# Both projections of a hybrid decoder layer as seven block products for eight, with heads one by one

## The chip, the cores and the metric

The kernel runs on one core of one Trainium2 chip. The metric is device time in microseconds (us) of one execution. Five engines work in parallel, each on its own queue of instructions: TensorE (PE, matrix products; its weight loads are shown as PEld), VectorE (DVE), ScalarE (ACT), GpSimd (POOL) and SyncE (SP, which here only issues DMAs). Sixteen DMA engines move the data that these queues ask for.

## The reference

One layer for 512 tokens and a model width of 2048, all in float32:

```python
h = rms_norm(x, norm_gain)
z = h @ w_in                        # 2048 -> 8192 columns, eight groups of 1024
q_h, f_h, i_h, g_h, q_a, k_a, v_a, g_a = split(z)
y_h = hgrn2_mixer(q_h, f_h, i_h) * silu(g_h)               # 8 heads of 128, chunks of 64 tokens
y_a = dilated_attention_mixer(q_a, k_a, v_a) * silu(g_a)   # 16 heads of 64
x = x + concat(y_h, y_a) @ w_out    # 2048 -> 2048
out = rms_norm(x, final_gain)
```

The HGRN2 mixer is a gated linear recurrence: a running product of the gates within a chunk, masked scores of 64 by 64, a state of 128 by 128 carried from chunk to chunk, and a norm per head. The attention is causal with a bias per head, and its three dilation patterns are merged into one count of how often a key is seen.

## The kernel before, in words

Each float32 operand of the two projections is cut in two float32r pieces: `hi` is a rounded copy (ScalarE) and `lo` the rest, source minus `hi` (VectorE, in places GpSimd). A product of two tiles is then three matmuls, hi by hi, hi by lo and lo by hi (`bank_step`, L134), each of a 128 x 128 stationary tile by 512 moving columns.

The 512 tokens' normed input stays in SBUF as 16 tiles `hh`, `hl` of 128 x 512, transposed (`split_h`, L174); the row norm is applied later, when a result leaves PSUM, so the products can start before it is known. It comes from squares that ScalarE makes and GpSimd adds up (`square_h`, `row_stats`, `row_stats_along`), while products run.

The columns of `w_in` are taken in chunks (L29): for each half of the HGRN heads the chunks `hq`, `hf`, `hg`, `hv` of 512 columns, that is four heads at a time, then for each half of the attention heads `av` with 512 columns and four chunks `ap` of 3 x 128 columns, one pair of heads each. A chunk is four (or three) PSUM banks filled over 8 weight tiles of 512 (384) KB, which are loaded on SP's queue five ahead (`load_w`) and cut three ahead (`split_w`). Values and gates of HGRN come out with tokens in the partitions, the rest with features there.

The mixers' work is strewn among the products: a `tick` stands ahead of each bank's share of a weight tile, and `at_slot(n, ...)` hangs a piece of a mixer on the n-th tick from there (`work_hf` and `work_hv` for HGRN, `work_ap` for a pair of attention heads). That is the order in the text; the framework's planner may still let a later instruction whose operands it expects to be ready go ahead of an earlier one on the same engine.

The mixers' outputs `yT` stay in SBUF, are cut (`split_y`) and go through `w_out` in two halves: first the eight HGRN tiles for all four column groups, then the eight attention tiles, each time four banks by 512 columns, with the residual `x` added when a bank is emptied. Squares for the last norm are taken group by group (`residual`), and the last 128 tokens are done in two halves of 256 columns so that the end is short (L657 to L663).

Of the kernel before, what the change touches and what calls it, by code (L numbers as in the profile page):

```python
# [8 lines left out]
F32 = mybir.dt.float32  # L9
# [4 lines left out]
PSUM = bass.MemoryType.PSUM  # L14

P = 128
S = 512
D = 2048
KT = D // P
NSB = S // P  # L20
HEADS_H = 8
HEADS_A = 16
CH = 64
# [5 lines left out]
def _chunks():  # L29
    out = []  # L30
    for g in range(2):
        for kind, base in (("hq", 0), ("hf", 1024), ("hg", 3072), ("hv", 2048)):
            out.append((kind, g, [(base + 512 * g, 512)]))
    for g in range(2):
        out.append(("av", g, [(4096 + 2048 + 512 * g, 512)]))
        for j in range(4 * g, 4 * g + 4):
            out.append(("ap", j, [(4096 + 128 * j, 128), (4096 + 1024 + 128 * j, 128),
                                  (4096 + 3072 + 128 * j, 128)]))
    return out


CHUNKS = _chunks()
# [3 lines left out]
def tile_kernel(ctx: ExitStack, tc: tile.TileContext, x, xT, w_in, w_out, gain, lbl, gnorm, fgain,  # L46
# [5 lines left out]
    wp = ctx.enter_context(tc.tile_pool(name="wp", bufs=2))  # L52
    pp = ctx.enter_context(tc.tile_pool(name="pp", bufs=4, space=PSUM))
    mx = ctx.enter_context(tc.tile_pool(name="mx", bufs=4, space=PSUM))
    yp = ctx.enter_context(tc.tile_pool(name="yp", bufs=1))

    def open_pool(name, side="left"):
        cm = tc.tile_pool(name=name, bufs=1, side=side)
        return cm, cm.__enter__()
# [4 lines left out]
    def mixer_bank(name):  # L64
        return mx.tile([P, 512], F32, tag="mx", name=name)

# [12 lines left out]


    offs = []
    o = 0
    for _, _, cols in CHUNKS:
        offs.append(o)
        o += 16 * P * sum(c for _, c in cols)

    stream = []
    for ci, (_, _, cols) in enumerate(CHUNKS):
        width = sum(c for _, c in cols)
        stream += [(w_in, offs[ci] + j * P * 2 * width, width) for j in range(8)]  # L90
    out_at = len(stream)
    out_order = [(n, j) for n in range(4) for j in range(4)] + [(n, j) for n in range(4) for j in range(4, 8)]
    stream += [(w_out, (n * 8 + j) * P * 2 * 512, 512) for n, j in out_order]
    raws, splits = [], []
    last_at = len(stream) - 4
    wl = {}

    def load_w(upto):
        while len(raws) < min(upto, len(stream)):
            i = len(raws)  # L100
            src, s0, width = stream[i]
            src = src[s0:s0 + P * 2 * width].rearrange("(p t c) -> p t c", p=P, t=2)
            raw = wp.tile([P, 2, width], F32, tag="raw", name=f"raw_{i}", bufs=5)
            if i == 0:
                nc.scalar.dma_start(raw[:, 0], src[:, 0])
                nc.sync.dma_start(raw[:, 1], src[:, 1])
            else:
                nc.sync.dma_start(raw, src)
            raws.append(raw)

    def split_w(upto):
        while len(splits) < min(upto, len(stream)):
            i = len(splits)
            width = stream[i][2]
            his, los = [], []
            for t in range(2):
                if i >= last_at:
                    hi = wl["pool"].tile([P, width], F32R, name=f"hi_{i}_{t}")
                    lo = wl["pool"].tile([P, width], F32R, name=f"lo_{i}_{t}")
                else:  # L120
                    hi = wp.tile([P, width], F32R, tag="hi", name=f"hi_{i}_{t}", bufs=6)
                    lo = wp.tile([P, width], F32R, tag="lo", name=f"lo_{i}_{t}", bufs=6)
                if i == 0:
                    V.tensor_copy(hi, raws[i][:, t])
                else:
                    A.copy(hi, raws[i][:, t])  # L126
                on_pool = i == 0 or (t == 1 and i < out_at and CHUNKS[i // 8][0] in ("hg", "hv"))
                (G if on_pool else V).tensor_sub(lo, raws[i][:, t], hi.bitcast(F32))  # L128
                his.append(hi)
                los.append(lo)  # L130
            splits.append((his, los))


    def bank_step(tokens_out, ps, b, k0, w, first, last, sh, sl, cols=slice(None)):  # L134
        c = slice(b * P, (b + 1) * P)
        for t in range(2):
            k, hi, lo = k0 + t, w[0][t][:, cols], w[1][t][:, cols]
            st_, en = first and t == 0, last and t == 1
            if tokens_out:
                T.matmul(ps, sh[k][:, c], hi, start=st_, stop=False)  # L140
                T.matmul(ps, sh[k][:, c], lo, start=False, stop=False)  # L141
                T.matmul(ps, sl[k][:, c], hi, start=False, stop=en)  # L142
            else:
                T.matmul(ps, hi[:, c], sh[k], start=st_, stop=False)  # L144
                T.matmul(ps, hi[:, c], sl[k], start=False, stop=False)  # L145
                T.matmul(ps, lo[:, c], sh[k], start=False, stop=en)  # L146
# [7 lines left out]

    yT = [yp.tile([P, S], F32, tag=f"y{k}", name=f"yT{k}") for k in range(8)]
    atv = ctx.enter_context(tc.tile_pool(name="atv", bufs=1))
    hp_cm, hp = open_pool("hp")
    hh, hl = [None] * KT, [None] * KT
    for k in reversed(range(KT)):
        hh[k] = hp.tile([P, S], F32R, tag=f"hh{k}", name=f"hh{k}")  # L160
        hl[k] = hp.tile([P, S], F32R, tag=f"hl{k}", name=f"hl{k}")
    st_cm, st = open_pool("st", "right")
    acc = st.tile([P, S], F32, name="acc")

    xts = []

    def load_x(upto):
        while len(xts) < min(upto, KT):
            k = len(xts)
            xt = st.tile([P, S], F32, tag="xt", name=f"xt_{k}", bufs=8)  # L170
            nc.sync.dma_start(xt, xT[k * P:(k + 1) * P, :])
            xts.append(xt)

    def split_h(k):  # L174
        xt = xts[k]
        A.activation(hh[k], xt, AF.Copy, scale=gain_sb[:, k:k + 1])  # L176
        V.scalar_tensor_tensor(hl[k], xt, gain_sb[:, k:k + 1], hh[k].bitcast(F32), op0=ALU.mult, op1=ALU.subtract)

    def square_h(k):
        if k == 0:  # L180
            A.activation(acc, xts[k], AF.Square)
        else:
            sq = st.tile([P, S], F32, tag="sq", name=f"xsq_{k}", bufs=3)
            A.activation(sq, xts[k], AF.Square)
            G.tensor_add(acc, acc, sq)

    cs = {}

# [12 lines left out]
    def small_consts():  # L201
        cc = cst.tile([P, 256], F32, name="cc")
        nc.sync.dma_start(cc, consts[:, :256])
# [6 lines left out]
        cs["gnorm"] = cst.tile([P, P], F32, name="gnorm_sb")  # L210
        nc.sync.dma_start(cs["gnorm"], gnorm[0:1, :].to_broadcast([P, P]))
        lt = cst.tile([P, 2, HEADS_H], F32, name="lt")
        nc.sync.dma_start(lt, lbl)
# [10 lines left out]
        cs["omlb"] = cst.tile([P, HEADS_H], F32, name="omlb")  # L224
        V.tensor_scalar(cs["omlb"], cs["lb"], -1.0, 1.0, op0=ALU.mult, op1=ALU.add)
        for name, half in (("hlb", 0.5), ("nhlb", -0.5)):
            cs[name] = cst.tile([P, HEADS_H], F32, name=name)
            V.tensor_scalar(cs[name], cs["omlb"], half, None, op0=ALU.mult)

    def row_stats():  # L230
# [9 lines left out]
        cs["hrstd"] = cst.tile([P, NSB], F32, name="hrstd")  # L240
        V.tensor_scalar(cs["hrstd"], rstd, 0.5, None, op0=ALU.mult)

    def row_stats_along():

        rstd = cs["rstd"]
        bank = mixer_bank("rrow_ps")
        for sb in range(NSB):
            dg = st.tile([P, P], F32, tag="dg", name=f"dg_{sb}", bufs=2)
            V.tensor_scalar(dg, cs["ident"], rstd[:, sb:sb + 1], None, op0=ALU.mult)
            T.matmul(bank[:, sb * P:(sb + 1) * P], cs["ones"], dg, start=True, stop=True)  # L250
        cs["rrow"] = cst.tile([P, S], F32, name="rrow")
        A.copy(cs["rrow"], bank)


    H = {}

    def open_hg():
        H["cm"], H["hg"] = open_pool("hg", "right")
# [6 lines left out]
    def evac_hq(g, banks):  # L265
        H["q"] = []
        for b, ps in enumerate(banks):
            q = H["hg"].tile([P, S], F32, tag="q", name=f"q_{g}_{b}", bufs=4)
            V.scalar_tensor_tensor(q, ps, 0.5, cs["rrow"], op0=ALU.mult, op1=ALU.mult)
            H["q"].append(q)  # L270
            at_slot(b + 1, silu, q, H["hg"], f"q_{g}_{b}")

    def silu(s, pool, name):

        t = pool.tile([P, S], F32, tag="t", name=f"t_{name}", bufs=2)
        A.activation(t, s, AF.Tanh)
        V.scalar_tensor_tensor(s, t, 1.0, s, op0=ALU.add, op1=ALU.mult)

    def evac_hf(g, banks):
        fs = []  # L280
        for b, ps in enumerate(banks):
            f = H["hg"].tile([P, S], F32, tag="f", name=f"f_{g}_{b}", bufs=4)
            V.tensor_mul(f, ps, cs["rrow"])
            fs.append(f)
        H["f"] = fs
        H["aux"] = [None] * 4
        for b in range(4):
            work_hf(g, b, H["q"][b], fs[b], H["aux"])

    def work_hf(g, b, q, f, aux):  # L290
# [444 lines left out]
```

## Time and profile before

| | us |
|---|---|
| median of 3 runs | 999.63 (999.51 to 1000.3) |
| the profiled execution | 999.73 |
| its span, first to last instruction | 998.0 |
| PE busy | 978.2 (98%) |
| DVE busy | 541.7 (54%) |
| ACT busy | 397.2 (40%) |
| POOL busy | 167.0 (17%) |

The page's first part gives busy time by engine. A busy PE is not PE at its peak: matmuls overlap, so the time that one costs is the distance from its start to the next start in the timeline, not its own duration. The chain of waits is followed back from the last instruction and says which engine's work set the end. The windows view gives busy time of each engine in a stretch, and the DMA part what the queues moved.

### The profile page before, as it was taken

The numbers are of one execution on the slowest core, as the hardware profiler recorded it, in microseconds if no ns is written. First come the engines' busy times: TensorE is split into PE (matmuls) and PEld (weight loads), VectorE is DVE, ScalarE is ACT, GpSimd is POOL, SyncE is SP. The second block draws the span as 40 slices with busy tenths as digits, with TensorE's granted clock in tenths as the row PEclk, the third lists the DMA queues.
The fourth block names the chain that finished last, engine by engine and source line by source line (L and its number), as shares of the span: only waits on it lengthen the run. The fifth ranks groups of instructions, "written<-read, shape, count | busy, mean of one in ns | idle before, by whom it ended". The sixth has DMA issues, their size and how long they took to land.

```text
span 998.0 us, 12703 instructions
## 1 busy us (share of the span) xinstructions
PE 978.2 (98%) x4704; PEld 799.6 (80%) x4704; DVE 541.7 (54%) x1107; ACT 397.2 (40%) x764; POOL 167.0 (17%) x150
## 2 busy tenths in 40 slices
PE   5999999999999999999999999999999999999996
PEld 4888888888888888888878778788787877888885
DVE  7752883245439813543765666326666686443533
ACT  5531543323334423242554454334444464213413
POOL 6500354011013620111000010000100100001220
PEclk8999999999999999999999999999999999999998
DMA  8422223311222332123222232133222362332304
GB/s 293 147 96 97 77 101 107 106 64 64 96 95 72 110 114 79 49 69 104 87 79 80 90 106 68 51 92 96 79 80 85 106 254 100 112 103 88 106 1 169
DMA packets 31486, 99.08 MB, mean 99 GB/s; under 512 B 3632, under 2 KB 3904, under 8 KB 30784
## 3 DMA queue, kind: packets, MB, share of 16 engines
q1 hardware_dynamic: 30528, 92.76, 28.2%
q0 software_dynamic: 752, 5.25, 1.3%
q8 instruction: 37, 0.61, 0.3%
q10 hardware_dynamic: 144, 0.26, 0.1%
q14 instruction: 25, 0.20, 0.1%
HBM read 94.06 MB, written 4.19 MB: 98 GB/s over the span
## 4 chain that ended last, share of the span: by engine, by line
PE 97%; ACT 1%; DVE 0%; DMA 0%; issue 0%; ACTq 0%; POOLq 0%; DVEq 0%
PE pp L144 15%; PE pp L146 15%; PE pp L145 14%; PE pp L140 9%; PE pp L142 9%; PE pp L141 9%; PE pq L140 3%; PE pq L142 3%; PE pq L141 3%; PE po L140 3%; PE po L141 3%; PE po L142 3%; PE ao L507 2%; PE p L498 2%; PE s L484 1%; PE s L483 1%
## 5 line engine op out<-in xcount | busy, mean ns | idle before, releaser
L128 DVE TENSOR_TENSOR lo<-raw,hi 128x512 fp32r<-128x512 f32 (+1 forms) x318 | 217.9, 695 | 266.9 <-ACT hi L126 215.8
L126 ACT CAST hi<-raw 128x512 fp32r<-128x512 f32 (+1 forms) x350 | 201.2, 581 | 377.2 <-PE pp L145 143.4
L144 PE MATMUL pp<-hh,hi 128*128 128x512 f32 x640 | 258.9, 406 | 6.3 <-ACT hh L176 6.1
L146 PE MATMUL pp<-hh,lo 128*128 128x512 f32 x640 | 251.7, 394 | 4.8 <-DVE lo L128 4.8
L145 PE MATMUL pp<-hl,hi 128*128 128x512 f32 x640 | 251.2, 393 | 0.0
L140 PE MATMUL pp<-hi,hh 128*128 128x512 f32 x384 | 152.2, 396 | 0.0
L142 PE MATMUL pp<-hi,hl 128*128 128x512 f32 x384 | 149.7, 390 | 0.0
L141 PE MATMUL pp<-lo,hh 128*128 128x512 f32 x384 | 149.6, 390 | 0.0
L146 PEld LDWEIGHTS pp<-hh,lo 128*128 128x128 f32 x640 | 121.2, 189 | 32.4 <-DVE lo L128 6.0
L144 PEld LDWEIGHTS pp<-hh,hi 128*128 128x128 f32 x640 | 121.6, 190 | 30.4 <-ACT hh L176 6.1
L145 PEld LDWEIGHTS pp<-hl,hi 128*128 128x128 f32 x640 | 121.9, 191 | 22.0
L142 PEld LDWEIGHTS pp<-hi,hl 128*128 128x128 f32 x384 | 72.1, 188 | 15.4
L140 PEld LDWEIGHTS pp<-hi,hh 128*128 128x128 f32 x384 | 72.1, 188 | 14.6 <-issue 0.3
L141 PEld LDWEIGHTS pp<-lo,hh 128*128 128x128 f32 x384 | 72.2, 188 | 13.8
L128 POOL TENSOR_TENSOR lo<-raw,hi 128x512 fp32r<-128x512 f32 x34 | 47.9, 1412 | 139.7 <-ACT hi L126 127.3
L489 ACT ACTIVATE pr<-pr,sm 128x128 f32<-128x128 f32 (+1 forms) x64 | 36.0, 563 | 72.2 <-DVE sm L487 72.2
L475 POOL TENSOR_SCALAR nb<-dist 128x512 f32<-128x512 f32 x16 | 9.9, 620 | 324.8 <-DVE sm L487 316.1
L140 PE MATMUL pq<-hi,yh 128*128 128x512 f32 (+1 forms) x136 | 52.0, 382 | 0.0
L141 PE MATMUL pq<-lo,yh 128*128 128x512 f32 (+1 forms) x136 | 52.0, 382 | 0.0
L142 PE MATMUL pq<-hi,yl 128*128 128x512 f32 (+1 forms) x136 | 52.0, 382 | 0.0
L140 PE MATMUL po<-hi,yh 128*128 128x512 f32 x128 | 51.0, 398 | 0.0
L142 PE MATMUL po<-hi,yl 128*128 128x512 f32 x128 | 49.9, 390 | 0.0
(153 smaller groups left out, 1098.8 us busy)
## 6 DMA issues: line engine op xcount, KB each, us to landing
raw<-w_in_dram SPq DMA_DIRECT2D x79, 512.0 KB, 3.3
raw<-w_in_dram SPq DMA_DIRECT2D x64, 384.0 KB, 3.0
raw<-w_out_dram SPq DMA_DIRECT2D x32, 512.0 KB, 3.3
xt<-xT_dram SPq DMA_DIRECT2D x16, 256.0 KB, 5.7
r<-x_dram POOLq DMA_DIRECT2D x4, 1024.0 KB, 8.9
out_dram<-r SPq DMA_DIRECT2D x16, 256.0 KB, 2.7
fg<-fgain_dram POOLq DMA_DIRECT2D x1, 1024.0 KB, 5.2
dist<-consts_dram SPq DMA_DIRECT2D x1, 512.0 KB, 4.5
```

The lines of the kernel that those rows point to most:

```text
L126: A.copy(hi, raws[i][:, t])
L128: (G if on_pool else V).tensor_sub(lo, raws[i][:, t], hi.bitcast(F32))
L140: T.matmul(ps, sh[k][:, c], hi, start=st_, stop=False)
L141: T.matmul(ps, sh[k][:, c], lo, start=False, stop=False)
L142: T.matmul(ps, sl[k][:, c], hi, start=False, stop=en)
L144: T.matmul(ps, hi[:, c], sh[k], start=st_, stop=False)
L145: T.matmul(ps, hi[:, c], sl[k], start=False, stop=False)
L146: T.matmul(ps, lo[:, c], sh[k], start=False, stop=en)
L483: T.matmul(s_ps[:, :L], Q[i][:, qc], KH[i][:, :L], start=True, stop=False)
L489: A.activation(p[:, :L], p[:, :L], AF.Exp, bias=sm[:, 0:1], scale=-1.0, accum_out=sm[:, 1:2])
L498: T.transpose(p_ps[:, c], pr[i, qb][:, c], cs["ident"])
L507: T.matmul(o_ps[64 * i:64 * i + 64, kb * P:], vs[kb][:, hc], PT[i][:, kb, kb * P:], start=kb == 0, stop=kb == 3)
```

## The change

The two projections are done by a scheme of Strassen's kind. Tokens are halved (2 x 256), the 2048 inner rows are halved, and the output columns are taken in pairs of blocks. A 2 x 2 by 2 x 2 block product then takes seven block products (m = 1 to 7) in place of eight, of sums and differences of the x blocks with sums of the weight blocks.

- *Units.* `w_in` is now taken in 32 units of two blocks of 128 columns: (f, q) and (v, g) for each of the 8 HGRN heads, (q, k) and (v, gate) for each of the 8 pairs of attention heads. So each head's or pair's mixer starts when its units end ("heads one by one"). Units 0 and 1 are done plainly, with eight products; the other 30 by seven.
- *x sums.* The x blocks X1, X2, X4 and A21, and the sums X7, X6, X5, X3 stay in SBUF as hi and lo tiles. X7 is made with the first unit, X5 and X6 during unit 1, X3 after it, in passes over 1024 columns per partition on VectorE.
- *Weight sums.* A buffer first gets one weight block by a plain DMA on SP's queue (`begin`), is used, and then gets the next block *added* by a DMA on GpSimd's queue (`grow`, `accum_op=ALU.add`): A holds W12, then adds W22 (m = 7), W11 (m = 6) and W21 (m = 4); B holds W11 (m = 1), then adds W12 (m = 5); C is W22 and D is W21. Each is 512 KB and is cut in two pieces of 128 x 512, four half products ahead.
- *Products.* A product is 2 x 4 x 3 matmuls of 256 moving columns; partial results go from PSUM into the z tiles by copies and adds over 256 columns. HGRN gates and values, which came out with tokens in the partitions, now come out transposed: values are turned by four transposes per head or pair, gates are applied after the turn back.
- *Output projection.* y goes to DRAM tiles and is read back, its sums are made on VectorE (`y_71` in the last unit, `y_2653` during the first output products, `y_4`), and `w_out` is taken in two column halves of seven products, each of 8 x 2 x 3 matmuls of 512 columns, with the same begin and grow of weight sums. The residual tiles take the place of result buffers.

The diff, cut to its core:

```diff
+ORDER = [(7, "A", "c", True), (1, "B", "a", True), (2, "D", "t", True), (6, "A", "a", False),
+         (3, "C", "t", True), (5, "B", "a", False), (4, "A", "c", False)]
+W11, W12, W21, W22 = (0, 0), (0, 1), (1, 0), (1, 1)
+FIRST = {"A": W12, "B": W11, "C": W22, "D": W21}
+GROW = {("A", 7): W22, ("A", 6): W11, ("A", 4): W21, ("B", 5): W12}
+NEXT = {("A", 7): 6, ("A", 6): 4, ("B", 1): 5}
...
+    def cut(hi, lo, src):
+        A.copy(hi, src)
+        V.tensor_sub(lo, src, hi.bitcast(F32))
...
+    def piece(name):
+        return tuple(wp.tile([P, 512], F32R, tag=p, name=f"{p}_{name}", bufs=5) for p in ("hi", "lo"))
...
+    def x5(t):
+        (h22, l22), (h21, l21) = whole(X[4], t), whole(A21, t)
+        d = D5[t] = H["dt"].tile([P, 4, HS], F32, tag="d5", name=f"d5_{t}")
+        V.tensor_sub(d, h22, h21)
+        V.tensor_add(d, d, l22)
+        V.tensor_sub(d, d, l21)
+        cut(*X[5][t], d)
...
+    W_BUFS = {"A": 2, "B": 1, "C": 1}
+
+    def begin(u, b):
+        t = "C" if b == "D" else b
+        r = wp.tile([P, 1024], F32, tag="w" + t, name=f"w{b}_{u}", bufs=W_BUFS[t])
+        raws[u, b] = r
+        nc.sync.dma_start(r, in_tile(u, FIRST[b]))
+
+    def grow(u, b, m):
+        nc.gpsimd.dma_start(raws[u, b], in_tile(u, GROW[b, m]), accum_op=ALU.add)
...
+    def cut_w(upto):
+        while len(cuts) < min(upto, len(steps)):
+            u, s, t = steps[len(cuts)]
+            m, b, _, _ = ORDER[s]
+            hi, lo = piece(f"{u}_{m}_{t}")
+            cut(hi, lo, raws[u, b][:, 512 * t:512 * t + 512])
+            cuts.append((hi, lo))
+            if t == 1:
+                if m == 2:
+                    begin(u, "C")
+                if (b, m) in NEXT:
+                    grow(u, b, NEXT[b, m])
+                elif u + 1 < len(UNITS) and b == "B":
+                    begin(u + 1, "B")
+                if u + 1 < len(UNITS):
+                    if m == 3:
+                        begin(u + 1, "D")
+                    if m == 6:
+                        begin(u + 1, "A")
+                        grow(u + 1, "A", 7)
...
+    def product(u, s, i0):
+        m, b, tag, opens = ORDER[s]
+        if opens:
+            banks[tag] = bank(tag, f"{tag}{m}_{u}")
+        ps = banks[tag][:, :HS]
+        for t in range(2):
+            tick()
+            cut_w(i0 + t + 4)
+            hi, lo = cuts[i0 + t]
+            xh, xl = X[m][t]
+            for kb in range(4):
+                c = slice(kb * P, kb * P + P)
+                st_, en = opens and t == 0 and kb == 0, t == 1 and kb == 3
+                T.matmul(ps, hi[:, c], xh[:, kb], start=st_, stop=False, skip_group_check=not opens)
+                T.matmul(ps, hi[:, c], xl[:, kb], start=False, stop=False, skip_group_check=not opens)
+                T.matmul(ps, lo[:, c], xh[:, kb], start=False, stop=en, skip_group_check=not opens)
...
+        elif m == 5:
+            for c in (slice(HS, S), slice(0, HS)):
+                V.scalar_tensor_tensor(z["z1"][:, c], ps, -1.0, z["z1"][:, c], op0=ALU.mult, op1=ALU.subtract)
...
+    def y_2653(kb):
...
+        h, a = staged(kb, "zB", zp, 2), staged(KH + kb, "zA", zp, 2)
+        a11, a21, a12, a22 = h[:, :HS], h[:, HS:], a[:, :HS], a[:, HS:]
+        y_cut(2, kb, a12)
+        V.tensor_sub(a21, a22, a21)
+        V.scalar_tensor_tensor(a11, a11, -1.0, a21, op0=ALU.mult, op1=ALU.subtract)
+        V.scalar_tensor_tensor(a22, a12, -1.0, a11, op0=ALU.mult, op1=ALU.subtract)
+        y_cut(6, kb, a11)
+        y_cut(3, kb, a22)
+        y_cut(5, kb, a21)
...
+    load_x(3)
+    load_plain(0, 0)
+    for u in range(PLAIN):
+        if u == 1:
+            for t in range(2):
+                at_slot(1 + 6 * t, x5, t)
+                at_slot(4 + 6 * t, x6, t)
...
+        plain_unit(u)
+    begin(PLAIN, "D")
+    for t in range(2):
+        x3(t)
```

## Rows read from the trace of the kernel before

**Rows 1.** Page, first part: span, and busy us with share and count.

```profile
span 998.0 us, 12703 instructions
PE 978.2 (98%) x4704; PEld 799.6 (80%) x4704; DVE 541.7 (54%) x1107; ACT 397.2 (40%) x764; POOL 167.0 (17%) x150
```

**Rows 2.** Page, the chain that ended last, by engine.

```profile
PE 97%; ACT 1%; DVE 0%; DMA 0%; issue 0%; ACTq 0%; POOLq 0%; DVEq 0%
```

**Rows 3.** Windows: stretch, its us, then busy us by engine, clock, DMA share.

```profile
105.00:150.00 45.00, 45.00 (x200) 37.24 (x200) 41.06 (x84) 22.13 (x36) 20.24 (x19) 1.00 0.27 91
254.77:446.41 191.64, 191.64 (x974) 159.52 (x972) 94.71 (x192) 68.58 (x113) 42.61 (x36) 1.00 0.26 85
517.02:557.34 40.32, 40.32 (x199) 32.22 (x200) 25.98 (x64) 19.11 (x44) 3.84 (x4) 1.00 0.26 79
```

**Rows 4.** Timeline of PE: start us, us, line, shape; 512 columns, in the input projection.

```profile
561.06 0.39 PE L144 MATMUL pp<-hh,hi 128*128 128x512 f32 x1
...
563.78 0.39 PE L144 MATMUL pp<-hh,hi 128*128 128x512 f32 x1
```

**Rows 5.** Timeline of PE near the end: 512 columns, then 256 columns.

```profile
975.10 0.40 PE L140 MATMUL pq<-hi,yh 128*128 128x512 f32 x1
...
981.87 0.39 PE L142 MATMUL pq<-hi,yl 128*128 128x512 f32 x1
...
983.50 0.28 PE L140 MATMUL pq<-hi,yh 128*128 128x256 f32 x1
...
989.04 0.28 PE L142 MATMUL pq<-hi,yl 128*128 128x256 f32 x1
```

**Rows 6.** Timeline of PE: first matmuls of the second chunk, first av, first ap.

```profile
62.98 0.50 PE L144 MATMUL pp<-hh,hi 128*128 128x512 f32 x1 [0.24 <-DVE q L269]
...
385.33 0.39 PE L140 MATMUL pp<-hi,hh 128*128 128x512 f32 x1
...
446.41 0.39 PE L144 MATMUL pp<-hh,hi 128*128 128x512 f32 x1
```

**Rows 7.** Lines by form: count, then busy us and mean ns, then idle time before.

```profile
L434 PE MATMUL y<-cc,os 128*128 128x128 f32 x32 | 4.8, 272 | 0.0
L128 DVE TENSOR_TENSOR lo<-raw,hi 128x512 fp32r<-128x512 f32 x190 | 146.1, 780 | 192.2 <-ACT hi L126 144.0 <-PE pp L145 47.5
L126 ACT CAST hi<-raw 128x512 fp32r<-128x512 f32 x222 | 135.6, 620 | 265.4 <-PE pp L142 92.8 <-PE pp L145 88.4 <-PE po L142 42.2
```

**Rows 8.** One line (L128, VectorE) in the second HGRN half: ns min/median/max.

```profile
L128 DVE TENSOR_TENSOR lo<-raw,hi x48: 551/692/1792, 254.9 to 442.3; 128x512 fp32r<-128x512 f32 x44, 128x384 fp32r<-128x384 f32 x4
```

**Rows 9.** Timeline of VectorE: two passes back to back.

```profile
123.62 0.41 DVE L327 TENSOR_TENSOR q<-p,q 128x256 f32<-128x256 f32 x1
123.96 0.41 DVE L329 TENSOR_TENSOR p<-p,q 128x256 f32<-128x256 f32 x1
```

**Rows 10.** Timeline of all engines at the start.

```profile
5.28 0.72 ACT L176 ACTIVATE hh<-xt,gain_sb 128x512 fp32r<-128x512 f32 x1 [2.63 <-DMA gain_sb<-gain_dram]
7.17 0.75 DVE L177 SCALAR_TENSOR_TENSOR hl<-xt,gain_sb,hh 128x512 fp32r<-128x512 f32 x1
8.38 9.70 DVE L177 SCALAR_TENSOR_TENSOR hl<-xt,gain_sb,hh 128x512 fp32r<-128x512 f32 x6 [0.46 <-ACT hh L176]
9.03 11.86 POOL L185 TENSOR_TENSOR acc<-acc,xsq 128x512 f32<-128x512 f32 x7
19.81 0.80 PE L146 MATMUL pp<-hh,lo 128*128 128x512 f32 x1 [4.80 <-DVE lo L128]
```

**Rows 11.** DMA queue (packets, MB, share of 16 engines); issues (KB each, us to landing).

```profile
q1 hardware_dynamic: 30528, 92.76, 28.2%
raw<-w_in_dram SPq DMA_DIRECT2D x79, 512.0 KB, 3.3
r<-x_dram POOLq DMA_DIRECT2D x4, 1024.0 KB, 8.9
fg<-fgain_dram POOLq DMA_DIRECT2D x1, 1024.0 KB, 5.2
```

More of the change, by code (lines that the diff above doesn't have):

```diff
@@ L22 @@
 HEADS_A = 16
+PAIRS = HEADS_A // 2
 CH = 64
@@ L94, in tile_kernel @@
[L94 to L131, printed above, removed]
@@ L134, in bank_step @@
[L134 to L146, printed above, removed]
+    def cut(hi, lo, src):
+        A.copy(hi, src)
+        V.tensor_sub(lo, src, hi.bitcast(F32))
@@ L153, in tile_kernel @@
     nc.gpsimd.dma_start(gain_sb, gain)
[L155 to L162, printed above, removed]
+    st_cm, st = open_pool("st")
     acc = st.tile([P, S], F32, name="acc")
@@ new lines, in plain_unit @@
+        for n, (kind, i, _) in enumerate(blocks):
+            z = block_tile(kind, i)
+            A.copy(z[:, :HS], banks[n][0][:, :HS])
+            V.tensor_copy(z[:, HS:], banks[n][1][:, :HS])
+            WORK[kind](i, z)
+    steps = [(u, s, t) for u in range(PLAIN, len(UNITS)) for s in range(7) for t in range(2)]
+    cuts = []
+    def cut_w(upto):
[18 more added lines that the diff above has]
+                        grow(u + 1, "A", 7)
@@ new lines, in tile_kernel, with staged, y_parts, y_cut @@
+    Y = {}
+    def staged(k, tag, pool, bufs):
+        s = pool.tile([P, S], F32, tag=tag, name=f"ys_{k}_{now[0]}", bufs=bufs)
+        nc.sync.dma_start(s, y_dram[k])
+        return s
+    def y_parts(m, kb):
+        t, b = divmod(kb, 4)
+        return tuple(a[:, b] for a in Y[m][t])
+    def y_cut(m, kb, src):
+        cut(*y_parts(m, kb), src)
+    def y_71(kb):
+        for m in (7, 1):
+            if m not in Y:
+                Y[m] = x_tiles(m)
+        h = staged(kb, "zA", zp, 2)
+        V.tensor_sub(h[:, HS:], h[:, :HS], h[:, HS:])
+        y_cut(7, kb, h[:, HS:])
+        y_cut(1, kb, h[:, :HS])
@@ new lines, in tile_kernel @@
+    O["late"] = []
+    at_slot(12, open_out)
+    for kb in range(KH - 1):
+        at_slot(1 + kb, y_2653, kb)
+    at_slot(13, y_2653, KH - 1)
+    i0 = 0
+    for u in range(2):
+        for s in range(7):
+            if u == 0 and s == 5:
+                for kb in range(KH):
+                    at_slot(1 + kb, y_4, kb, ("zB" if kb % 2 else "zA", zp, 2))
+            o_product(u, s, i0)
+            i0 += KH
+            if u == 1 and s == 1:
+                open_out2()
+    assert not cal, sorted(cal)
```

885 lines of the change are left out of this document (535 added, 350 removed).

## The prediction

> **What bounds the kernel now.** I read the page's first part, then the chain of waits, then windows by stage, then starts in the timeline. The reader is to see that PE is busy 98% of a span of 998.0 us [rows 1] and that the chain runs through PE for 97% of it [rows 2]: the products alone set the time. VectorE has 54% of the span, but it is no bystander, since nearly everything that this change adds lands on it. Its share differs by stage: 41.06 of 45 us where four heads' gate work falls together, with PE still busy for all 45, and 25.98 of 40.32 us in a pair of attention heads [rows 3]. So a stage can carry VectorE at 91% while PE does not wait.
>
> What a matmul costs is the distance between starts. 512 columns: 12 distances from 561.06 to 563.78, 0.2267 us each [rows 4]; in the last quarter 29 from 975.10 to 981.87, 0.2334 us [rows 5]. 256 columns with a new stationary tile each time: 47 from 983.50 to 989.04, 0.1179 us [rows 5], half of the 0.2334 beside it plus 1.2 ns. In the faster stretches I expect 0.1145 (half of 0.2267, plus that). So narrow matmuls keep the rate per column, and weight loads don't get in the way.
>
> **PE, part by part.** Before, the products are 3072 + 768 matmuls of 512 columns. After, 30 units x 168 = 5040 of 256 columns, 2 plain units x 192 = 384 of 256, and 2 x 7 x 48 = 672 of 512. Columns fall to 0.881 of before; at 0.2267 that is some 100 us of 870.
>
> Mixers' matmuls stay. Per HGRN head: the first av chunk, among whose matmuls four heads' mixers run, takes 61.08 us [rows 6] for 192 matmuls (43.5) and these heads, 4.4 us each. Per pair: 40.32 us [rows 3] for 144 matmuls (32.6), 7.7 us. New are 4 transposes per head or pair; 32 such take 4.8 us by busy time [rows 7], so at most 0.15 each and not below nothing; with overlap I take 0.11, 0.45 us a head. A head's two units of seven products are 336 x 0.1145 = 38.5 us. So a head costs PE 38.5 + 4.4 + 0.45 = 43.3 us and a pair 46.6 us. Seven heads and the rest of head 0: 308 us; eight pairs: 373 us; output 672 x 0.23 = 154.5 us.
>
> **VectorE beside it.** From the second hf chunk to the first av chunk VectorE is busy 94.71 us [rows 3], of which 48 cuts of about 0.7 are 34 [rows 8]: 15 us for each of four heads, and 1 more for q, whose chunk lies ahead. The change adds per head eight result passes over 256 columns (0.41 each, 0.34 from start to start [rows 9]), 3 us, and 28 cuts of 128 x 512 at 0.65 (from 0.61, what the dense step of 0.34 gives for twice the columns with 0.07 of overhead once, to the mean of 0.78 [rows 7]; the median is 0.69 [rows 8]), 18 us: 37 to 39 us in 43.3. A pair has 25.98 us [rows 3] less its 16 cuts of 384 columns (0.55, the least in [rows 8]), 17 us; after it 17 + 3 + 18, less 1 us that goes to ScalarE: 37 us in 46.6. Both are under the 91% that PE bore. ScalarE has 19.11 us in a pair [rows 3], 11 without cuts, and gets 28 x 0.6 [rows 7] and 5 us of copies: 33. These costs I count as hidden; what they cost without cover is a rival below.
>
> **The start is where the cover is gone.** Before, the second chunk starts at 62.98 us [rows 6] after 43.5 us worth of products. After, two plain units hold 45 us of products, but VectorE must first do this. Unit 0: 48 passes over 256 columns (splits and X7) at 0.38, 18 us, with GpSimd adding squares beside them: six such passes over 512 took 9.70 us in that company and 0.75 each alone [rows 10], twice as much; I take 1.5 times, 27 us, and 8 cuts, 5 us, from the first landing at 5.3 us [rows 10]: end at 38. The row norm is no longer spread over the last banks but stands between the units: 6 us. Unit 1 and X3: X5, X6 and X3 are 22 passes over 1024 columns, at 1.2 us (0.41 and 0.69 for 256 and 512 [rows 8, 9], so 0.28 per 256 more) 26 us, and 17 us of cuts, gate work of head 0 and results. The first product of unit 2 stands behind all of it, at about 88 us. PE waits some 10 us just before; after an idle stretch of 4.80 us the next matmul took 0.80 us [rows 10] where 0.39 is usual [rows 4], so PE comes back slow, and I add 2 us: 90. Bounds: 80 if the passes run dense and alone, 103 if all are slowed as in [rows 10].
>
> **The change-over to the output.** From the last unit through the first two output products VectorE has 30 cuts (20 us), 80 passes over 256 columns for the y sums (30 us), 19 us of the last pair and 3 us of results: 72 us, against 50 us on PE. Less 6 us that the cuts are ahead, 16 us are lost; between 5 (dense) and 24. On SP's queue a head's store of y waits for its last VectorE pass and holds the weight loads behind it; these wait for later cuts anyway. The staged loads of y come in four and more ticks before their use, and VectorE, already late, hides them. The end after the last matmul stays at 998.0 - 989.0 = 9 us.
>
> **Adding DMAs.** No row shows one. A sum in A is cut at half product 1, grown, and cut again at 6; again at 7 and 12 of 14. Five half products of 1.55 us less the cut itself leave 6.6 us. A plain 512 KB takes 3.3 us, 1024 KB on GpSimd's queue 5.2, and 8.9 with four in flight [rows 11]. Queueing adds about 1 us. Below: as the plain one, 4.3, and nothing waits. Above: 9.9, 3.3 us late, twice per unit, 30 units: 198 us. I take the row nearest to twice the bytes, 6.2: in time, with scatter of 0.7 us per unit, 20 us. What would queue behind a late one: ScalarE's copy and VectorE's difference of that cut, with the mixers' work behind them; and on GpSimd's queue the carry products of a head behind the wait of `grow`.
>
> Here a page of the Trainium skill bears on it: DMA: Bandwidth & Descriptors, section Anatomy of one DMA, gives 2.0 us + bytes / 436 GB/s for a DMA of GpSimd's queue, an estimate of 3.2 us for 512 KB and 4.4 us if an addition counts its bytes twice; the row of 1024 KB has 5.2 where that rule gives 4.4. By the rule nothing is late, and the sum below would be 20 us less.
>
> **Sum.** 90 + 308 + 373 + 154.5 + 16 + 9 = 950.5, with 20 us of scatter 970. The profiled execution took 999.73 with a span of 998.0, so 1.7 us lie around it, and it stands 0.1 us over the median: 972.
>
> **Rivals.**
> 1. Adding DMAs come late (slower than before). Place: the second and third cut of A in each of the 30 units, and again in the output. Price: each us beyond 6.6 costs 2 us per unit, 60 us; it passes the time of before from 0.5 us of lateness over the scatter (950 + 20 + 30). For it: a unit moves 8 x 512 KB in 21.7 us, 193 GB/s where the queue's rate at full share is 92.76 MB / 0.282 of 998 us = 330 GB/s [rows 11]; if an addition counts twice it is 290 GB/s, 88%, and transfers queue. Against: the sums in B and the next A have two half products more. One us late gives 1032. The Trainium skill has a rule to this effect (SBUF — State Buffer, section SBUF: two separate sides): while VectorE runs an operation that takes both of its port pairs, GpSimd can't write the descriptors of its DMAs. No row before shows a GpSimd DMA beside such work.
> 2. VectorE becomes the bound: if the mean 0.78 us per cut [rows 7] holds and its waits on ScalarE and PE in a pair aren't filled with other work, a head takes 46 and a pair 50 us in place of 43.3 and 46.6: 46 us more than the sum without scatter, and some 15 us with it, 1012. For it: VectorE goes from 54% to near 85% of the span. Against: 41.06 of 45 us without a wait of PE [rows 3].
> 3. All hidden: start at 80 us, change-over 5, no scatter: 931 to 945, say 940.
> 4. That narrow matmuls don't keep their rate, so that nothing is saved, is excluded by [rows 5].
>
> **How the numbers follow.** The forecast 0.50, own range 950 to 998; late DMAs 0.22, from 1000 up to 1090; VectorE bound 0.13, 995 to 1030; all hidden 0.15, 930 to 950. About 0.2% (2 us) is what a measurement here can tell from no change. Faster: 0.46 + 0.15 + 0.03 = 0.64; within 0.2%: 0.05; slower 0.31. Range 938 to 1035: above it some 0.09, of late DMAs; below some 0.06.
>
> **What would show it.** PE: starts of 256 columns 0.114 to 0.118 us apart in the units. First matmul of unit 2 near 90 us. Windows of a head's two units near 43 us and of a pair's near 47 once running, VectorE busy at 85 to 90% there. A wait of ScalarE's cut for a DMA on the weight sums, over 1 us and several per unit, would show rival 1; PE waiting for `lo` of VectorE with no DMA late, rival 2. PE idle 15 us around the first output products. The forecast is wrong if units take over 24.5 us throughout.

## The result and the profile after

The changed kernel takes 1074.6 us (median of 4 runs, 1071.12 to 1078.29), the kernel before 999.7 beside it: a ratio of 1.0749, 95% interval 1.0712 to 1.0785. The forecast was 972 us, with a range up to 1035: wrong in sign and size. The profiled execution took 1074.24 us, its span is 1072.5.

The page of the changed kernel (busy time by engine, share of the span, instructions; then the chain of waits by engine):

```profile
PE 954.5 (89%) x7000; PEld 889.5 (83%) x7000; DVE 768.2 (72%) x1536; ACT 584.6 (55%) x1250; POOL 245.5 (23%) x259
...
PE 37%; DMA 27%; DVE 19%; ACT 9%; issue 6%; POOL 1%; SPq 0%; ACTq 0%; DVEq 0%; POOLq 0%
```

The reader is to see two things against [rows 1] and [rows 2]. PE is busy for fewer microseconds, but it no longer sets the end: its part of the chain fell from 97% to 37%, and transfers, which had no part, hold 27%. And VectorE, to which nearly all the added work went, is at 72%, so it has room.

The waits of the changed kernel (engine, line, for whom: us in total, times, longest):

```profile
DVE lo L108 <- ACT hi L107: 158.2, 131, 5.0
ACT hi L107 <- DMA wA<-w_in_dram: 78.1, 31, 4.5
ACT hi L107 <- DMA wC<-w_in_dram: 62.2, 28, 5.1
```

ScalarE's cut waits for the sums in A, as rival 1 said, but nearly as long for C, which is loaded by a plain DMA. The DMA view answers [rows 11] (queue, packets, MB, share of 16 engines; then issues, count, size, median us to landing):

```profile
q0 software_dynamic: 22624, 81.95, 42.8%
q1 hardware_dynamic: 36576, 108.02, 29.9%
...
wA<-w_in_dram POOLq DMA_DIRECT2D x90, 512.0 KB, 5.8
...
wD<-w_in_dram SPq DMA_DIRECT2D x30, 512.0 KB, 3.7
wB<-w_in_dram POOLq DMA_DIRECT2D x30, 512.0 KB, 8.6
wC<-w_in_dram SPq DMA_DIRECT2D x30, 512.0 KB, 5.8
```

q0 is GpSimd's queue with the adding DMAs: 81.95 MB in 0.428 x 1072.5 = 459 us of all engines, 178 GB/s; SP's plain loads move at 337 GB/s. C and D are both plain and of one size; D lands after 3.7 us, C after 5.8. The difference is what runs beside them: of the 30 loads of C, the 11 that were issued with three adding DMAs in flight landed after a median of 8.0 us, the 10 with one after 4.3.

One such place, in head 6, first GpSimd's issues, then SP's, ScalarE and PE (timeline: start, us, engine, line, out<-in, shapes, idle before and its releaser):

```profile
342.87 1.77 POOL L576 DMA_DIRECT2D wA<-w_in_dram  x2
344.98 0.86 POOL L576 DMA_DIRECT2D wB<-w_in_dram  x1 [0.33 <-DVE lo L108]
...
347.03 0.33 SPq L573 DMA_DIRECT2D wC<-w_in_dram  x1
...
355.16 0.62 ACT L107 CAST hi<-wC 128x512 fp32r<-128x512 f32 x1 [4.29 <-DMA wC<-w_in_dram]
355.68 0.37 ACT L709 COPY f<-a 128x256 f32<-128x256 f32 x1
...
356.10 0.39 PE L700 MATMUL a<-X6h,hi 128*128 128x256 f32 x1 [2.25 <-ACT f L709]
```

Three adding DMAs leave within 2.1 us and land 5.5, 8.3 and 10.4 us after their issue; C, issued 2 us after the last, needs 8.0. The first is the sum for m = 6; by its operands it could have left 1.5 us earlier, but GpSimd was still on passes of the mixer (L361 to L363). The second is already the sum for the next unit's m = 7, which the planner lets go here, ahead of its place in the text; in 21 of 29 units these two leave within 1.5 us of each other. ScalarE stands at C's cut for 4.29 us, and behind it on its queue stands the copy of product m = 1 out of PSUM (L709), for which PE's next product waits 2.25 us. PE comes back at its usual distance, but 1.2 us later the granted clock falls (windows: busy us and count by engine, granted clock, DMA share, GB/s):

```profile
357.30:360.70 3.40, 3.40 (x19) 3.40 (x18) 2.62 (x5) 1.07 (x3) 0.00 (x0) 0.51 0.44 101
360.80:364.00 3.20, 3.20 (x29) 3.20 (x28) 2.18 (x5) 1.13 (x3) 0.00 (x0) 1.00 0.70 233
```

From 357.3 to 360.7 us 1.2 GHz is granted, with 19 matmuls; in the 3.2 us after it, at 2.4 GHz, there are 29. So this late load cost its wait and, by the clock, some 1.7 us more. By the mean granted clock (0.959, and 0.993 before) some 88 us of the run lie at the lower level, where the kernel before has 14.

By stage: the first product of unit 2 starts at 87.5 us (forecast 90); the 30 units take 760.8 (701 with scatter); from the first output product at 848.3 to the end 224.1 (179.5). The units lost 60 us against the forecast, the output 45.

### The profile page after: what moved, and what is told of

Read it like the earlier page. It is cut to its first block, busy times and chain, and to the rows that moved or that the text cites. A ratio compares the mean times of both kernels' runs of the same rounds, so it can differ in the third digit from the quotient of the medians.

```text
span 1072.5 us, 18864 instructions
## 1 busy us (share of the span) xinstructions
PE 954.5 (89%) x7000; PEld 889.5 (83%) x7000; DVE 768.2 (72%) x1536; ACT 584.6 (55%) x1250; POOL 245.5 (23%) x259
## 3 DMA queue, kind: packets, MB, share of 16 engines
q0 software_dynamic: 22624, 81.95, 42.8%
## 4 chain that ended last, share of the span: by engine, by line
PE 37%; DMA 27%; DVE 19%; ACT 9%; issue 6%; POOL 1%; SPq 0%; ACTq 0%; DVEq 0%; POOLq 0%
DMA wA<-w_in_dram 11%; DMA wC<-w_in_dram 7%; DVE lo L108 5%; PE a L700 4%; PE a L701 3%; PE a L702 3%; ACT hi L107 2%; PE t L700 2%; PE t L702 2%; PE t L701 2%; PE ao L539 2%; DMA wB<-w_in_dram 2%; DMA r<-x_dram 2%; DMA ys<-yd 2%; PE oa L954 2%
## 5 line engine op out<-in xcount | busy, mean ns | idle before, releaser
L108 DVE TENSOR_TENSOR lo<-wA,hi 128x512 fp32r<-128x512 f32 x180 | 127.7, 712 | 106.9 <-ACT hi L107 101.7
L107 ACT CAST hi<-wA 128x512 fp32r<-128x512 f32 x180 | 109.7, 618 | 147.0 <-DMA wA<-w_in_dram 78.1
L576 POOL DMA_DIRECT2D wA<-w_in_dram x90 | 79.2, 932 | 429.6 <-DVE lo L108 297.6
L107 ACT CAST hi<-wB 128x512 fp32r<-128x512 f32 x120 | 73.0, 618 | 43.2 <-PE a L701 20.2
L700 PE MATMUL a<-X6h,hi 128*128 128x256 f32 x240 | 73.1, 305 | 20.2 <-ACT f L709 15.7
L108 DVE TENSOR_TENSOR lo<-wB,hi 128x512 fp32r<-128x512 f32 x120 | 86.0, 730 | 0.3
L107 ACT CAST hi<-wC 128x512 fp32r<-128x512 f32 x60 | 35.7, 617 | 64.4 <-DMA wC<-w_in_dram 62.2
L700 PE MATMUL t<-X2h,hi 128*128 128x256 f32 x240 | 70.7, 295 | 0.0
L702 PE MATMUL a<-X6h,lo 128*128 128x256 f32 x240 | 70.6, 294 | 0.0
L701 PE MATMUL a<-X6l,hi 128*128 128x256 f32 x240 | 70.6, 294 | 0.0
L700 PE MATMUL a<-X1h,hi 128*128 128x256 f32 x240 | 70.4, 293 | 0.0
```

The costliest lines, as they stand in the source:

```text
L107: A.copy(hi, src)
L108: V.tensor_sub(lo, src, hi.bitcast(F32))
L576: nc.gpsimd.dma_start(raws[u, b], in_tile(u, GROW[b, m]), accum_op=ALU.add)
L700: T.matmul(ps, hi[:, c], xh[:, kb], start=st_, stop=False, skip_group_check=not opens)
L701: T.matmul(ps, hi[:, c], xl[:, kb], start=False, stop=False, skip_group_check=not opens)
L702: T.matmul(ps, lo[:, c], xh[:, kb], start=False, stop=en, skip_group_check=not opens)
```

## The experiments

The kernel before ran beside all of them: 998.6 to 1000.3 us. Those with one execution are read against a spread of some 4 us either way, as the changed kernel shows it.

**1. The same transfers without the addition.**

```diff
-        nc.gpsimd.dma_start(raws[u, b], in_tile(u, GROW[b, m]), accum_op=ALU.add)
+        nc.gpsimd.dma_start(raws[u, b], in_tile(u, GROW[b, m]))
```

(and in `o_grow` the same)

> Every DMA that adds a weight block to a buffer becomes a plain load of the same block into the same buffer, from the same queue (GpSimd's), with the same waits; so the weight sums are left out and the output is another. Theory A (the additions in the DMAs cost the time: 81.95 MB on that queue take 42.8% of the engines, 1.8 times a plain byte, and loads of C and ScalarE's queue stand behind them): the DMA share in the units falls from 0.76 to under 0.62, a head's two units from 50 to about 46 us, a pair's from 50 to 49, the output phase from 224 to about 190 us, in all 990 to 1015 us. Theory B (VectorE and ScalarE and the round trips between them are the bound, whatever the DMAs do): 1055 us or more.

Measured 996.57 us, span 994.8. The same bytes, on the same queue, in the same order:

```profile
q0 software_dynamic: 22624, 81.95, 25.9%
...
wA<-w_in_dram POOLq DMA_DIRECT2D x90, 512.0 KB, 4.1
```

258 us of all engines in place of 459: adding makes a transfer 1.78 times as long for the engines. 77.7 us come back, 57 in the units (760.8 to 703.9) and 20 in the output (224.1 to 203.7). That is theory A; the output came back less than it said (203.7 for 190). GpSimd's issue takes 546 ns in place of 932. Since 4.1 us on GpSimd's queue is near the 4.0 of SP's queue for A beside it, the queue itself is not the cause.

**2. No second loads at all.**

```diff
-        nc.gpsimd.dma_start(raws[u, b], in_tile(u, GROW[b, m]), accum_op=ALU.add)
+        pass
```

> The second and later loads into a weight buffer are left out altogether, so the cuts read the first block again and the output is another; the instructions of the other engines are the same. Theory A: units are bound by PE, 20.2 us of matmuls and 4 to 8 us of mixers per head or pair, output phase about 185 us, in all 975 to 995 us. Theory B: 1050 us or more, since VectorE and ScalarE have the same work. If this is over 20 us below the run with plain loads, bytes count and not only the additions.

Measured 985.53 us: theory A. The units, 709 us, are no shorter than with plain second loads; the output is, 186.2. So these bytes were free in the units and cost 17 us in the output.

**3. What narrow matmuls cost, in the kernel before.**

```diff
-                T.matmul(ps, hi[:, c], sh[k], start=st_, stop=False)
-                T.matmul(ps, hi[:, c], sl[k], start=False, stop=False)
-                T.matmul(ps, lo[:, c], sh[k], start=False, stop=en)
+                for x, y, s_, e_ in ((hi, sh, st_, False), (hi, sl, False, False), (lo, sh, False, en)):
+                    for a in range(n):
+                        m = slice(256 * a, 256 * a + 256)
+                        T.matmul(ps[:, m], x[:, c], y[k][:, m], start=s_, stop=e_, skip_group_check=True)
```

(n is 2 for 512 columns; likewise where tokens come out in the partitions)

> The kernel before, with each matmul of 512 moving columns of both projections done as two of 256 columns with the same stationary tile: the price of narrow matmuls by itself, without the rest of the change. Theory M (each matmul costs 32 cycles beyond its columns, 13.3 ns: 0.2267 us for 512 and 0.120 for 256): 3840 times 13 ns more, 1040 to 1055 us. My forecast's reading (cost goes by columns, 1.2 ns more for a matmul): 1003 to 1008 us.

Measured 1039.42 us, 40.7 us over the kernel before beside it: theory M, 0.6 us under its range. Its timeline in the stretch of [rows 4]:

```profile
561.11 0.40 PE L155 MATMUL pp<-hh,lo 128*128 128x256 f32 x2
561.35 0.40 PE L155 MATMUL pp<-hh,hi 128*128 128x256 f32 x2
561.59 0.40 PE L155 MATMUL pp<-hl,hi 128*128 128x256 f32 x2
561.83 0.40 PE L155 MATMUL pp<-hh,lo 128*128 128x256 f32 x2
```

Two halves take 0.24 us where one matmul of 512 columns took 0.2267: 0.120 each. From the two widths a column is 0.417 ns here and each matmul has 13.3 ns on top. It isn't so everywhere: over the whole run the 3816 more matmuls cost 10.7 ns each. In the second half of the output, where [rows 5] lie, the wide ones take 0.2334 us and the narrow ones 0.118, so that splitting adds next to nothing; why the wide ones are slower there, no run shows. The changed kernel's units have the same distance:

```profile
409.79 0.28 PE L701 MATMUL t<-X3l,hi 128*128 128x256 f32 x1
...
411.23 0.28 PE L701 MATMUL t<-X3l,hi 128*128 128x256 f32 x1
```

12 distances of 0.120; the mean over all units is 0.1197, so 5040 matmuls cost 26 us more than at 0.1145.

**4. Two buffers for C and D.**

```diff
-    W_BUFS = {"A": 2, "B": 1, "C": 1}
+    W_BUFS = {"A": 2, "B": 1, "C": 2}
```

(paid for with one `pr` buffer and a tile of the output's A)

> The changed kernel with two buffers for the weight blocks C and D in place of one, so that C needn't wait for the cuts of D (to make room, one buffer less of the attention's probabilities, and one output tile elsewhere). Theory A in its narrow form (C, loaded late beside adding DMAs, is what ScalarE waits for: 62 us): waits for wC nearly gone, units 1.5 us shorter each, 1025 to 1045 us. If the adding DMAs of A (78 us of waits) set the pace by themselves: 1060 us or more. Theory B: unchanged, 1070 to 1078 us.

Measured 1057.57 us, between the two. The waits for C are gone, those for A rose from 78.1 us:

```profile
ACT hi L107 <- DMA wA<-w_in_dram: 119.7, 44, 4.5
```

Giving C its load earlier moved part of the lateness to the sums.

**5. The sums by GpSimd's own additions.**

```diff
+    def grow(u, b, m, t):
+        a = raws[u, "A", t]
+        if m == 5:
+            G.tensor_sub(raws[u, "B", t], a, raws[u, "C", t])
+        else:
+            G.tensor_add(a, a, raws[u, {7: "C", 6: "B", 4: "D"}[m], t])
```

> Weight sums made by GpSimd additions of 128 x 512 instead of by adding DMAs. In the units W22, W11 and W21 are taken from the buffers that hold them anyway (the sum for m = 5 as the sum for m = 6 minus W22), so each block is loaded once, by a plain DMA; in the output projection the second blocks come by plain loads into two spare 128 x 512 tiles (the first four sums there still by adding DMAs). Theory A (the addition inside the DMA is what costs, and loads by themselves keep up): units near those of the kernel without second loads, 708 to 720 us from 88 us on, output 200 to 215 us, total 985 to 1012 us. Rival G (8 additions of 1.41 us per unit slow VectorE beside them, as GpSimd's additions went with slow VectorE passes at the start, and VectorE becomes the bound): units of 25 us or more, total 1035 to 1080 us.

Measured 1125.18 us: rival G, and beyond it. VectorE's cuts, in the changed kernel and then here (line, engine, operation, out<-in, shapes, count, busy us, mean ns, idle before):

```profile
L108 DVE TENSOR_TENSOR lo<-wA,hi 128x512 fp32r<-128x512 f32 x180 | 127.7, 712 | 106.9 <-ACT hi L107 101.7 <-PE a L701 4.5
...
L108 DVE TENSOR_TENSOR lo<-wC,hi 128x512 fp32r<-128x512 f32 x60 | 45.0, 770 | 56.2 <-ACT hi L107 55.8
```

```profile
L108 DVE TENSOR_TENSOR lo<-wA,hi 128x512 fp32r<-128x512 f32 x180 | 150.6, 843 | 38.4 <-ACT hi L107 38.1
...
L108 DVE TENSOR_TENSOR lo<-wC,hi 128x512 fp32r<-128x512 f32 x60 | 77.3, 1303 | 4.9 <-ACT hi L107 4.7
```

The DMA engines were at a share of 0.28 here, from 200 to 440 us, and no cut of ScalarE in the units waited for a load; but a cut of VectorE beside an addition takes up to 1.3 us by the mean in place of 0.77, and VectorE is busy for 969.9 us. The Trainium skill (SBUF — State Buffer, section Who interferes with whom) says that a VectorE instruction with two inputs in SBUF gets one of them through a port that it shares with GpSimd, and waits while GpSimd reads; these rows agree.

**6. Adding DMAs of half the size.**

```diff
+            if (b, m) in NEXT:
+                grow(u, b, NEXT[b, m], t)
```

(each half, 256 KB, as soon as it is cut)

> The changed kernel with each adding DMA of the units issued as two of 128 x 512, each as soon as its half of the sum is cut; the output projection is as it was. Theory L (one adding DMA of 512 KB has too long a latency for the time between two cuts of A): the first half starts some 1.5 us earlier, waits of ScalarE's cut for A and C shrink, total 1040 to 1060 us. Theory E (the time that additions take on the DMA engines delays all loads beside them, whenever and in whatever size they are issued): total 1065 to 1090 us, and the waits for C stay.

Measured 1079.5 us: theory E by the time. The 180 halves for A land after 5.8 us by the median, as the whole ones did. Waits of ScalarE's cuts in this kernel:

```profile
ACT hi L107 <- DMA wC<-w_in_dram: 83.2, 29, 6.2
ACT hi L107 <- DMA wA<-w_in_dram: 33.2, 26, 3.1
```

The waits for A did shrink, from 78.1 us, as theory L had it; but those for C grew from 62.2, and nothing was won. Smaller pieces queue for the same engines.

**7 and 8. Half of the additions each.**

```diff
+        op = {} if m in (6, 4) else dict(accum_op=ALU.add)
+        nc.gpsimd.dma_start(raws[u, b], in_tile(u, GROW[b, m]), **op)
```

(in the other kernel `m in (7, 5)`)

> The changed kernel, but in the units the second and third weight sums in A (m = 6 and 4, five half products from cut to cut) are plain loads that don't add (these two sums are left out); those for m = 7 and 5, which have more time, still add, and so does the output projection. Theory T (what costs is the lateness of the two tight sums): units back to 23.0 to 23.5 us on average as with plain loads, total 1012 to 1025 us. Theory R (an adding DMA moves its bytes at a fraction of the rate of a plain one, so that the transfers of a unit together nearly fill the queues, and every addition taken away gives back about its share): half of the units' 57 us, total 1030 to 1048 us.

> The other half: the sums for m = 7 and 5 in the units are plain loads that don't add (left out), those for m = 6 and 4 still add, and so does the output projection. Theory T: nearly nothing comes back, total 1060 to 1072 us. Theory R: as the kernel beside it, total 1030 to 1048 us.

Measured 1066.14 and 1042.69 us. Theory T is refuted, the wrong way round: with the two tight sums plain only 8 us come back, with the two loose ones 32. Theory R holds for the second and fails for the first; the parts don't add. What each kernel's C says of it, first with the tight sums plain, then with the loose ones plain:

```profile
ACT hi L107 <- DMA wC<-w_in_dram: 77.5, 28, 6.0
```

```profile
ACT hi L107 <- DMA wC<-w_in_dram: 33.9, 23, 2.4
```

33.9 us is what the plain loads of experiment 1 have (34.3). C has three half products, 4.65 us less a cut, for a load of 3.6 us, and both loose additions, which need no haste themselves, go out ahead of it: in the place shown above that for m = 5 2.1 us before C, that for the next unit's m = 7 3.6 us. The waits for C fell by 28 us, the time by 32. Which of the two additions costs more, this run doesn't separate.

**9. Additions spread out.**

```diff
-                if (b, m) in NEXT:
-                    grow(u, b, NEXT[b, m])
+                if b == "A" and m != 4:
+                    grow(u, b, NEXT[b, m])
+                elif m == 2:
+                    grow(u, "B", 5)
                 elif u + 1 < len(UNITS) and b == "B":
                     begin(u + 1, "B")
...
                     if m == 3:
                         begin(u + 1, "D")
+                        grow(u + 1, "A", 7)
```

(on top of experiment 4)

> The kernel with two buffers for C and D (1057.6 us), and with the adding DMAs of a unit issued one by one: that for m = 5 after the cut for m = 2 instead of m = 1, that for the next unit's m = 7 after the cut for m = 3 instead of m = 6, where it goes out together with the one for m = 4. Each has then at least five half products. Theory B (they are late because two or three are issued at once): waits of ScalarE's cut for A fall by half or more, total 1030 to 1048 us. Theory R (their rate alone fills the time): total 1050 to 1062 us.

Measured 1086.27 us, 29 slower than experiment 4, which neither theory had. But the edit does more than the text above says: its last branch is now reached at m = 1 as well as at m = 5, so a unit loads the next unit's B twice. The plain loads of B, in experiment 4 and then here:

```profile
wB<-w_in_dram SPq DMA_DIRECT2D x30, 512.0 KB, 4.4
```

```profile
wB<-w_in_dram SPq DMA_DIRECT2D x59, 512.0 KB, 4.3
```

That is 29 more loads, 15.2 MB. Waits for A are 95.0 us; those for B rose from 17.6 to 55.3, 30 us of them at m = 1, whose block comes by a plain load. Nor were the additions spread: 25 of 120 left within 1.5 us of the one before, 22 in experiment 4. So this run doesn't tell whether bunching is part of the cause; that stays open.

**10. Two of the four sums on VectorE.**

```diff
+            if m in (7, 6):
+                c = slice(512 * t, 512 * t + 512)
+                w = raws[u, "A"][:, c]
+                V.tensor_add(w, w, raws[u, "B" if m == 7 else "D"][:, c])
```

(on top of experiment 4; W11 and W21 are in B and D anyway, so two second loads go)

> The kernel with two buffers for C and D, in which the sums for m = 6 and 4 are made on VectorE from the blocks in B and D that are there anyway (two additions of 128 x 512 each, 2.8 us per unit by the 0.69 us of a cut), without second loads; those for m = 7 and 5 stay adding DMAs, and the output projection is as in the changed kernel. Theory R: two adding DMAs in a unit no longer fill the queues, units 22.5 to 24 us on average, total 1015 to 1035 us. Rival V (VectorE, at some 39 of 45 us in a head, becomes the bound with 5.5 us more): units of 25 us or more, total 1055 us or more.

Measured 1027.5 us: theory R for the units. Windows over 200 to 440 us of the changed kernel and of this one:

```profile
200.00:440.00 240.00, 222.81 (x1869) 219.28 (x1865) 168.54 (x344) 125.09 (x257) 50.87 (x55) 0.98 0.76 176
```

```profile
200.00:440.00 240.00, 240.00 (x2077) 238.10 (x2076) 209.34 (x418) 138.10 (x279) 41.12 (x43) 1.00 0.62 147
```

PE is busy for all 240 us with VectorE at 87%; the cuts of all units wait 2.3 us in total for loads. Of the 60 adding DMAs that are left one leaves within 1.5 us of another, and they land after 5.5 us by the median. The units are through at 802.6 us; the output still takes 223.

**11. Another order in the output.**

```diff
+    O_ORDER = [[ORDER[1], ORDER[0]] + ORDER[2:], ORDER]
...
+            if s == 1:
+                c = slice(512 * half, 512 * half + 512)
+                w = oraw[u, "A", jb][:, c]
+                V.tensor_add(w, w, oraw[u, "B", jb][:, c])
```

> The kernel with two sums per unit on VectorE (1027.5 us), and in the output projection: the first half's products in the order m = 1, 7, 2, ..., so that the one whose weights need no sum comes first, and in both halves the sum for m = 6 on VectorE from the block in B, in place of an adding DMA. Theory R (the first three output products, 72 us for 33 us of matmuls with the DMA engines full at a share of 0.8 to 1.0, are held up by adding DMAs): these three at 50 to 60 us, total 1003 to 1016 us. Rival V (there VectorE's work on the y sums sets the time, whatever the DMAs do): no change, 1022 to 1032 us.

Measured 1022.93 us, in rival V's range near its lower edge: the first three products still take 67 us, and the first starts 8 us later. Which of VectorE, the reads of y and the loads holds them up, this run doesn't tell.

**12 and 13. A version without what cost.** Units as in experiment 10, `PLAIN = 3`, and the output by eight products:

```diff
+    def o_pass(p):
+        kh, u, n = passes[p]
+        banks = [o_bank(p, sb, f"o_{p}_{sb}") for sb in range(NSB)]
+        for kb in range(KH):
+            for sb in range(NSB):
...
+                o_step(p, sb, kb, banks[sb])
+        for sb in range(NSB):
+            residual(kh, u, n, sb, banks[sb])
```

> A version that drops what cost: units with two of the four sums on VectorE (as in the run whose units followed PE alone), three plain units in place of two so that PE has products while VectorE makes the x sums, and an output projection of eight plain products with 512 columns, by eight column groups without adding DMAs. Theory R: first output product near 790 to 800 us, output 190 to 198 us with its end, total 980 to 998 us, below the kernel before. Rival V (the change-over stays bound by VectorE even without the y sums, or the third plain unit does not fill the wait at the start): output over 205 us or units no earlier than with two plain units, total 1002 us or more.

> The same kernel as the one look before (984.21 us), timed in five rounds. If the units' gain is real: 982 to 987 us, a ratio of 0.983 to 0.988 to the kernel before. If that execution was a lucky one: 992 us or more.

Measured 984.21 us, and as the median of 4 further runs 985.39 us (983.26 to 987.5) beside 999.27: a ratio of 0.9863, interval 0.9842 to 0.9883. That is theory R, and the gain is real: 1.4% less than the kernel before. Its page:

```profile
PE 945.3 (96%) x7144; PEld 893.8 (91%) x7144; DVE 776.8 (79%) x1540; ACT 548.4 (56%) x1172; POOL 171.4 (17%) x169
...
q0 software_dynamic: 9088, 32.66, 19.7%
...
PE 80%; DVE 8%; DMA 4%; ACT 3%; issue 3%; POOL 1%; POOLq 0%; ACTq 0%; DVEq 0%
```

The chain is PE's again. Unit 3 starts at 109.5 us, where experiment 10 with two plain units had it at 121.7: PE has products while VectorE makes the x sums. The output takes 189.7 us from its first product, where experiment 10 took 223. The changes came together; what each gives by itself is not shown beyond these two stages.

## Why the prediction was wrong

**Adding DMAs: the step that failed.** It took 6.2 us for one from twice the bytes of a plain one, set that against 6.6 us between two cuts of A, and called it in time, with 20 us of scatter. The duration was near: with next to nothing beside it one takes 5.3 to 6.0 us (experiment 10), and the median for A is 5.8. (The rule of the Trainium skill, DMA: Bandwidth & Descriptors, section Anatomy of one DMA, gave an estimate of 3.2 or 4.4 us; the trace has more.) Two things were missing.

First, the 6.6 us were a mean. In experiment 2, where no cut waits for a second load, ScalarE's next cut of A starts 5.2 us after the end of the cut before it for m = 6 and 7.4 for m = 4 in the first unit of a head, 9.6 and 2.8 us in the second (medians). So sums that landed after 5.5 us (m = 6) and 5.9 us (m = 4) were in time by the forecast, and yet ScalarE waited 46.6 and 31.5 us for them.

Second, transfers share engines. Rival 1 had the sum for that, 88% of the queues if an addition counts twice; the runs give 1.78 times: four adding DMAs of 2.95 us and four plain ones of 1.56 are 18.0 us of engine time in a unit of 21.7. At 83% loads wait for each other, and the step that was waited for most was no sum at all but C, 62.2 us, a plain load with 4.65 us to spare, for which I worked out no limit. So 20 us of scatter stood for what was 57 us in the units and 20 in the output (experiment 1).

**Rival 1** was the case that came: 1074 lies in its span of 1000 to 1090, to which I gave 0.22. Its place was only half right: it named the second and third sum in A; without these two additions 8 us come back, without the other two 32, with 28 us less of waits for C (experiments 7 and 8). The rule of the Trainium skill on starved descriptors, cited beside it (SBUF — State Buffer, section SBUF: two separate sides), has no support here: with VectorE at 77%, plain loads on GpSimd's queue land after 4.1 us, on SP's after 4.0 (experiment 1).

**What a matmul costs** failed by 0.005 us: I scaled the 256 columns of [rows 5] by the ratio of the two 512-column distances in [rows 4, 5], as if narrow matmuls gained in the faster stretches what wide ones do. They don't: 256 columns take 0.118 to 0.120 us in both stretches of experiment 3. So rival 4, which [rows 5] were to exclude, held in part: two narrow ones take 0.24 us for 0.2267. That is 26 us of the miss in the units; experiment 2, without any sums, shows the forecast's 681 us as 709.

**The start** was right in its number, 87.5 us for 90, and only in part in its path, so some of that is luck. The 22 passes over 1024 columns take 1.2 us each, as forecast. But X3, which was to stand ahead of unit 2, ran beside it, from 84.4 to 98.8 us; PE waited 7.8 us inside unit 1 instead, for a cut behind X5 and X6, and unit 2 took 27.5 us in experiment 2 where later units of its kind take 24.4.

**VectorE** had room, as forecast: in experiments 2 and 10 PE is busy for 239.6 and 240.0 of 240 us with VectorE at 77 and 87%, so rival 2 is refuted in the units. For the change itself 85 to 90% were forecast, and experiment 2 has 77. A head of 43.3 us measured 45.1, a pair of 46.6 measured 47.9 (experiments 1 and 2), within 0.5 us of what the width of 336 matmuls adds.

**The change-over** was mis-sized. Without second loads the first three output products take 53.4 us for 32.6, a loss of 21 where 16 were forecast; with them 69.1. The output's second loads cost 17 us there as plain ones and 20 more by adding, where I had counted both at nothing: the reads of y, the residual and the weight loads meet in those 70 us, where the changed kernel's DMA share is 0.80 to 1.06.

## What to carry to other kernels

Price a new kind of transfer twice: by its own latency against its own deadline, and by the time that it takes on the shared DMA engines; then write down the deadline of every load that it will stand beside, the plain ones first, and the shortest of a loop's deadlines, not their mean. An in-order engine that does both the cuts and the PSUM copies turns one late load into a wait of PE. Take the cost of a matmul's width from the stretch in which it will run; scaled over from another it was 5% off here. And compare an experiment's DMA counts with those of the kernel that it builds on, as experiment 9 shows.

## What the runs showed of the hardware

- An adding DMA of 512 KB with next to nothing beside it (others in flight for less than a quarter of its time) landed after 5.3 to 6.0 us (19 in experiment 10), a plain one on the same queue after 3.8 to 4.4 (10 in experiment 1). Its bytes move at 178 GB/s of full share, plain ones on the same queue at 318.
- A plain load of 512 KB landed after a median of 8.0 us where three adding DMAs were in flight at its issue, after 4.3 where one was (C in the changed kernel).
- GpSimd is busy for 932 ns with the issue of an adding DMA, 546 ns with that of a plain one of the same shape.
- In the input projection matmuls of 256 and 512 columns start 0.120 and 0.2267 us apart: 13.3 ns that don't depend on the width. In the second half of the output they start 0.118 and 0.2334 us apart.
- A difference of VectorE beside GpSimd's additions of the same size took 0.84 to 1.30 us by the mean of a group, for 0.70 to 0.77.
